# The two ends of a feed-forward's first products: token halves, order of the last transposes, and how the next product's accumulators are taken

## The chip, the cores and the metric

One core of one Trainium2 chip runs the whole program. The time is the device time of one execution in microseconds; the kernel before and the changed one compute the same function from the same inputs.

## What is computed

One layer for 512 tokens of width 1024, in float32: a mixer of four groups, a cross-attention to 256 memory rows, and a gated feed-forward of width 2816, each behind a norm and added back to x. Only the last part is touched, with the norm in front of it:

```python
def conv_glu_ffn(xn, w_up, conv_w, conv_b, w_down):
    gu = xn @ w_up                                   # 1024 -> 2 x 2816
    gate, up = jnp.split(gu, 2, axis=-1)
    gate = causal_dwconv(gate, conv_w) + conv_b      # 3 taps over the tokens
    return (jax.nn.silu(gate) * up) @ w_down         # 2816 -> 1024
...
h = conv_glu_ffn(rmsnorm(x, norm_ffn_pre[l]), ...)
x = x + rmsnorm(h, norm_ffn_post[l])
```

## The kernel before

The 512 tokens are four token tiles t of 128, the 2816 features 22 feature tiles f of 128. Every large product is done with operands split into a high and a low part (`split`, L484: a ScalarE copy that rounds to the high part, then a VectorE subtraction for the low part), three matmuls for one: high x high, high x low, low x high (`three`).

Order. Nothing in the kernel is in the order in which the code is written. Each call records an operation with an engine, a modelled cost, its dependencies and the buffers that it takes; `Plan.schedule` then lays all of them out with a greedy list scheduler, and `issue` emits them in that order. So every engine runs a fixed queue, in order, that the planner's model chose, and waits where the real times differ. The rules that matter here:

- Among the operations of an engine that are ready at the same planned time, the one with the largest `bl + boost` goes first (L275). `bl` is the longest modelled path from the operation to the end, `boost` is set by hand around pieces of code. A DMA ignores it.
- Operations stand in units (`pl.unit`). A unit starts only when the buffers that it needs can all be promised to it, and when every unit that it depends on has started (`est`, L235). PSUM has 8 banks (L40).
- A matmul into a PSUM bank depends on every earlier operation that touched that bank.

The feed-forward's norm. For each token tile t, after the cross-attention and its residual (`residual`, L1043), `norm_T` (L573) takes the squares of x on ScalarE, a power of -1/2 on GpSimd (`rr`), a scaled copy on VectorE (`xs`), eight TensorE transposes, a ScalarE copy that keeps a float32 version (`xf`), and the split into `xTh` and `xTl`. For t = 2 and 3 sums and differences of the kept tiles follow (`xf`, `Th`, `Tl`), with a boost of -60000.

First products. A feature tile is either `plain` (L1175; gate and up, 2 x 8 x 3 matmuls of 512 columns) or `seven` (L1241; a scheme of seven block products in place of eight, 7 x 12 matmuls of 256 columns, into two banks a and b, from sums of weight blocks that `blocks` forms on ScalarE and VectorE). `PLAIN` (L34) lists the plain tiles: 0, 1, 2, 6, 11, 16. Tile 0 is done by token halves: its matmuls have 256 columns, and those of the tokens of t = 0 and 1 come before those of t = 2 and 3. Tile 1 reads all four token tiles in each matmul. In a seven, S1, S3, S2 and S4 are products with sums of weight blocks, G1, G2 and U2 with plain blocks; G2 reads a bank that was first copied out (`c1`), S4 and U2 one that was copied out as `c57`. `glu` (L1164) makes the gated result `hT` from a finished tile.

Second product. Each `hT` is split into `hh` and `hl` (L1284), not before `ups[-2]`, which is what `seven(20)` returns: its product U2. The down product accumulates over the 22 feature tiles into eight banks `od[t][c]`. For f = 0 all eight stand in one unit, and its matmuls may not come before `up_`, the U2 of tile 21. The loads of x for the last residual and of the last gain wait for the same U2.

Of the kernel before, what the change touches and what calls it, by code (L numbers as in the profile page):

```python
# [30 lines left out]
NT = S // P  # L31
DFF = 2816
NF = DFF // P
PLAIN = (0, 1, 2, 6, 11, 16)  # L34
EPS = 1e-6
NEG = -1e30

# [305 lines left out]
def kernel(  # L343
# [134 lines left out]
    def tpose(o, a, idn, n=None):  # L478
        return pl.op("PE", 109.0, lambda: nc.tensor.transpose(o.ap(), a.ap(), idn.ap()), reads=[a, idn], writes=[o])  # L479
# [92 lines left out]
    @unit  # L572
    def norm_T(src, g, dst, keep=None):  # L573
        xs = [sb([P, 512], FT, "xs") for _ in range(2)]
        r = rms([src[:, h * 512:(h + 1) * 512] for h in range(2)], xs)
        for h in range(2):
            hs = slice(h * 512, (h + 1) * 512)
            stt(xs[h].all, src[:, hs], r[:, 0:1], g[:, hs], OP.mult, OP.mult)
        for h in range(2):
            p = ps([P, 4, P])  # L580
            for k in range(4):
                tpose(p[:, k, :], xs[h][:, k * P:(k + 1) * P], idn)
            if keep:
                act(keep[h], p.all, AF.Copy)
            split(*dst(h), p.all)

    def into(t):
        return lambda h: (xTh[:, t, 4 * h:4 * h + 4], xTl[:, t, 4 * h:4 * h + 4])
# [509 lines left out]
    for t in range(NT):  # L1098
# [27 lines left out]
        with pl.unit():  # L1126
            pp = []
            for c in range(2):
                p, cs = ps([P, 512]), slice(c * 512, c * 512 + 512)
                for k in range(4):  # L1130
                    wh, wl = wo[k]
                    mms(p.all, three(oh_[:, k, :], ol_[:, k, :], wh[:, 0, cs], wl[:, 0, cs]), k == 0, k == 3,
                        spare=BIG)
                pp.append(p)
            xo2 = residual(pp, g_cpost, t)
        if t < 2:
            xf.append([sb([P, 4, P], FT, "xf") for h in range(2)])
            norm_T(X[t], g_fpre, into(t), [b.all for b in xf[t]])
        else:
            with pl.unit():  # L1140
                b1, b2 = [sb([P, 4, P], FT, "xf") for h in range(2)]
                norm_T(X[t], g_fpre, into(t), [b1.all, b2.all])
                a1, a2 = xf[t - 2]
                i = t - 2
                pl.boost -= 60000.0

                tt(a1.all, b1.all, a1.all, OP.subtract)
                tt(b1.all, b2.all, b1.all, OP.subtract)
                tt(b2.all, b2.all, a1.all, OP.subtract)
                tt(a2.all, a2.all, b2.all, OP.subtract)  # L1150
                for j, v in enumerate((a1, b2, b1, a2)):
                    split(Th[j][:, i], Tl[j][:, i], v.all)
                pl.boost += 60000.0
        kept.append(store(flat(x2, t * P * D, [[D, P], [1, D]]), X[t].all, P * D * 4))


# [18 lines left out]
    def plain(f):  # L1175
        ww = [stage(wsrc(w_ffn_in, 0, KT, j * DFF + f * P, P), [P, KT, P], 8 if f < 2 else 4) for j in range(2)]
        with pl.unit():
            pp = []
            for j in range(2):
                p = ps([P, S])  # L1180
                wh, wl = ww[j]
                for hv_ in [slice(0, 2), slice(2, 4)] if f < 1 else [slice(0, 4)]:
                    for k in range(KT):
                        o = mms(p[:, hv_.start * P:hv_.stop * P],
                                three(wh[:, k, :], wl[:, k, :], xTh[:, hv_, k, :], xTl[:, hv_, k, :]),
                                k == 0, k == KT - 1)
                pp.append(p)
            glu(f, pp[0], pp[1].all)
        return o

    def raw(f):
        with pl.unit():
# [48 lines left out]
    def seven(f):  # L1241
        W = blocks(*raw(f))
        with pl.unit():
            a, b = ps([P, 2, 256]), ps([P, 2, 256])

            def prod(o, w, xs, first):
                return mms(o, [q for i in range(4) for q in three(W[w][0][i], W[w][1][i], *xs[i])], first, n=256, open_=True)
            prod(b[:, 0], "S1", tblock(0), True)
            prod(b[:, 1], "S3", tblock(2), False)
            prod(a[:, 0], "G1", xblock(0, 0), True)  # L1250
            prod(a[:, 1], "S2", tblock(1), False)
            c57 = sb([P, 2, 256], FT, "c57")
            act(c57.all, b.all, AF.Copy)
            prod(b[:, 0], "S4", xblock(1, 1), False)
            o = prod(b[:, 1], "U2", tblock(3), False)
            c1 = sb([P, 256], FT, "c1")
            act(c1.all, a[:, 0], AF.Copy)
            prod(a[:, 0], "G2", xblock(1, 0), False)
# [4 lines left out]
            tt(c57[:, 0], c57[:, 0], c57[:, 1], OP.add)  # L1263
            tt(gu[:, 768:], c1.all, c57[:, 0], OP.add)
            glu(f, gu, gu[:, S:])
        return o

    ups = [plain(f) if f in PLAIN else seven(f) for f in range(NF)]
    up_ = ups[-1]

    g_fpost = gain(norm_ffn_post, [up_])
    NL = 3
    wd, hT = [], []
    for f in range(NF):
# [6 lines left out]
            wd.append((hb.all, lb2.all))  # L1281
        with pl.unit():
            hh, hl = sb([P, S], FR, "hh", kind="hh"), sb([P, S], FR, "hl")
            act(hh.all, hP[f // 2][:, f % 2, :], AF.Copy, quota=[("hh", 4)], after=[ups[-2]])  # L1284
            tt(hl.all, hP[f // 2][:, f % 2, :], hh.all.cast(FT), OP.subtract)
            hT.append((hh, hl))

# [6 lines left out]
    od = [[ps([P, 512]) for c in range(2)] for t in range(NT)]  # L1294
    for t in range(NT):
        X[t] = sb([P, D], FT, "X2")
        load(X[t].all, flat(x2, t * P * D, [[D, P], [1, D]]), P * D * 4, after=[kept[t], up_])
    for f in range(NF - NL):
        with pl.unit():
            for t in range(NT):  # L1300
                for c in range(2):
                    down(od[t][c].all, f, t, c)
# [120 lines left out]
```

## Time and profile before

| | us |
|---|---|
| median of 3 runs (lowest to highest) | 748.5 (746.23 to 749.05) |
| the profiled execution's own time | 747.11 |
| its span, first to last instruction | 745.3 |

An execution's time is the span and what lies around it, 1.81 us here. The engines are named PE (TensorE's matmuls), PEld (its weight loads), DVE (VectorE), ACT (ScalarE), POOL (GpSimd) and SP (the queue that issues the DMAs). A matmul's recorded duration is that of a pipelined instruction; what one costs is the distance between the starts of two in a row. Line L462 is the helper `mms` for every matmul but the transposes (L479), L387 is `act`, L400 is `tt`, L412 is `stt`, L565 the power in `rms`. Tiles are told by their names: `p` is any PSUM tile, `c` is `c1` or `c57`, `su`, `sh`, `sl`, `uh` and `ul` belong to `blocks`.

### The profile page before, as it was taken

Reading aid. Unit: us, or ns where it says so; the run is one execution under the profiler, and the core shown is the slowest. Engines: PE = TensorE matmul, PEld = TensorE weight load, DVE = VectorE, ACT = ScalarE, POOL = GpSimd, SP = SyncE. Lnnn points to the kernel's source line nnn. Section 1 sums busy time; section 2 is a strip of 40 time slices with the busy share of each in tenths; the row PEclk is TensorE's granted clock in tenths of the full one; section 3 lists DMA queues with packets and bytes.
Section 4 is the critical chain, followed back from the end, with each engine's and each line's share of the span. In section 5 each row is a group of like instructions: output and inputs, shape, how many; then the busy total and the mean of one; then the engine's idle time right before and its main releaser. Section 6 shows DMA issues by size and latency. Waiting matters only on the chain.

```text
span 745.3 us, 11908 instructions
## 1 busy us (share of the span) xinstructions
PE 727.7 (98%) x4614; PEld 647.4 (87%) x4614; DVE 522.6 (70%) x1007; ACT 389.1 (52%) x790; POOL 35.5 (5%) x65
## 2 busy tenths in 40 slices
PE   7999999999999999999999999999999989999996
PEld 6898989998887988889887999999999988888885
DVE  5889956785674646676888679898979997334105
ACT  6794347546574545465666355463655565324102
POOL 3000210011000001000010000000000000000001
PEclk9999999999999999999999999999999999999999
DMA  8800320410325543333134043052234146441003
GB/s 300 299 1 1 130 93 29 173 55 28 112 116 163 163 155 103 123 113 121 51 118 166 29 142 114 29 179 77 77 126 134 34 161 235 141 150 49 0 1 113
DMA packets 25696, 82.07 MB, mean 110 GB/s; under 512 B 2980, under 2 KB 4644, under 8 KB 25640
## 3 DMA queue, kind: packets, MB, share of 16 engines
q1 hardware_dynamic: 25352, 80.72, 31.9%
q8 instruction: 36, 0.59, 0.3%
q0 software_dynamic: 288, 0.59, 0.3%
q14 instruction: 20, 0.16, 0.1%
HBM read 77.10 MB, written 4.20 MB: 109 GB/s over the span
## 4 chain that ended last, share of the span: by engine, by line
PE 85%; DVE 7%; ACT 5%; issue 2%; DMA 1%; POOL 0%; SPq 0%; DVEq 0%; POOLq 0%; ACTq 0%
PE p L462 81%; PE p L479 3%; DMA st<-in_w_in_dram 1%; PE p L474 1%; ACT wh L387 1%; DVE at L428 1%; DVE wl L400 1%; DVE Qt L400 0%; ACT e L387 0%; POOL rr L565 0%; DVE xTl L400 0%; DVE X L412 0%; DVE pg L400 0%; DVE E L400 0%; DVE sl L400 0%
## 5 line engine op out<-in xcount | busy, mean ns | idle before, releaser
L462 PE MATMUL p<-xTh,wh 128*128 128x512 f32 (+1 forms) x432 | 147.4, 341 | 2.5 <-ACT c L387 2.0
L462 PE MATMUL p<-xTl,wh 128*128 128x512 f32 (+1 forms) x432 | 145.7, 337 | 0.7 <-DVE xTl L400 0.7
L462 PE MATMUL p<-xTh,wl 128*128 128x512 f32 (+1 forms) x432 | 145.3, 336 | 0.0
L400 DVE TENSOR_TENSOR wl<-st,wh 128x1024 fp32r<-128x1024 f32 (+3 forms) x101 | 118.7, 1190 | 29.8 <-ACT wh L387 29.7
L387 ACT ACTIVATE wh<-st 128x1024 fp32r<-128x1024 f32 (+3 forms) x101 | 101.5, 1029 | 8.5 <-DMA st<-in_w_in_dram 5.8
L462 PEld LDWEIGHTS p<-xTh,wh 128*128 128x128 f32 x432 | 81.7, 189 | 10.8 <-ACT c L387 2.4
L462 PEld LDWEIGHTS p<-xTh,wl 128*128 128x128 f32 x432 | 81.7, 189 | 9.3
L462 PEld LDWEIGHTS p<-xTl,wh 128*128 128x128 f32 x432 | 81.8, 189 | 8.4 <-DVE xTl L400 1.1
L462 PE MATMUL p<-wh,xTh 128*128 128x256 f32 (+1 forms) x192 | 56.5, 294 | 0.2 <-ACT xTh L387 0.2
L462 PE MATMUL p<-wh,hh 128*128 128x512 f32 x144 | 56.7, 394 | 0.0
L462 PE MATMUL p<-wh,hl 128*128 128x512 f32 x144 | 56.7, 394 | 0.0
L462 PE MATMUL p<-wl,hh 128*128 128x512 f32 x144 | 56.7, 394 | 0.0
L462 PE MATMUL p<-wh,xTl 128*128 128x256 f32 (+1 forms) x192 | 54.0, 281 | 0.4 <-DVE xTl L400 0.4
L462 PE MATMUL p<-wl,xTh 128*128 128x256 f32 (+1 forms) x192 | 54.1, 282 | 0.0
L462 PE MATMUL p<-Th,sl 128*128 128x256 f32 x192 | 54.0, 281 | 0.0
L462 PE MATMUL p<-Th,sh 128*128 128x256 f32 x192 | 53.9, 281 | 0.0
L462 PE MATMUL p<-Tl,sh 128*128 128x256 f32 x192 | 53.9, 281 | 0.0
L400 DVE TENSOR_TENSOR hl<-hT,hh 128x512 fp32r<-128x512 f32 x22 | 15.1, 690 | 52.8 <-ACT hh L387 52.8
L387 ACT ACTIVATE hh<-hT 128x512 fp32r<-128x512 f32 x22 | 13.8, 629 | 64.2 <-PE p L462 64.2
L565 POOL TENSOR_TENSOR rr<-rv,mhalf 128x1 f32<-128x1 f32 x26 | 15.8, 608 | 568.5 <-DVE rv L407 565.0
L462 PEld LDWEIGHTS p<-wh,xTh 128*128 128x128 f32 x192 | 36.2, 189 | 1.0 <-ACT xTh L387 0.5
L400 DVE TENSOR_TENSOR pg<-p,gain 128x512 f32<-128x512 f32 x24 | 16.4, 685 | 29.1 <-ACT sq L387 29.1
(281 smaller groups left out, 1760.9 us busy)
## 6 DMA issues: line engine op xcount, KB each, us to landing
st<-in_w_ffn_in_dram SPq DMA_DIRECT2D x44, 512.0 KB, 4.5
st<-in_w_in_dram SPq DMA_DIRECT2D x24, 512.0 KB, 4.3
st<-in_w_ffn_out_dram SPq DMA_DIRECT2D x22, 512.0 KB, 3.7
st<-in_w_mix_out_dram SPq DMA_DIRECT2D x8, 512.0 KB, 4.6
st<-in_w_ck_dram SPq DMA_DIRECT2D x4, 512.0 KB, 9.1
st<-in_w_cv_dram SPq DMA_DIRECT2D x4, 512.0 KB, 3.9
X<-in_x_dram SPq DMA_DIRECT2D x4, 512.0 KB, 3.9
st<-in_w_cq_dram SPq DMA_DIRECT2D x4, 512.0 KB, 3.9
```

The source lines that it names most:

```text
L387: return nc.scalar.activation(o.ap(), i.ap(), func, **kw)
L400: return pl.op(eng, c, lambda: e.tensor_tensor(o.ap(), a.ap(), b.ap(), op=op), reads=[a, b], writes=[o], fifo=fifo, boost=boost)
L428: return pl.op("DVE", dcost(n, True), lambda: nc.vector.copy_predicated(o.ap(), m.ap(), a.ap()), reads=[m, a, o], writes=[o])
L462: i = nc.tensor.matmul(o.ap(), l.ap(), r.ap(), start=first and j == 0, stop=last and j == len(terms) - 1, skip_group_check=open_)
L474: i = nc.tensor.matmul(o[hh * 64:hh * 64 + 64].ap(), l.ap(), r.ap(), start=j == 0, stop=j == len(terms) - 1)
L479: return pl.op("PE", 109.0, lambda: nc.tensor.transpose(o.ap(), a.ap(), idn.ap()), reads=[a, idn], writes=[o])
L565: pl.op("Pool", 470.0, lambda: nc.gpsimd.tensor_tensor(r.all.ap(), v.all.ap(), mhalf[:, :1].ap(), op=OP.pow), reads=[v.all, mhalf.all], wr ...
```

## The change

- `PLAIN` is 0, 1, 2, 6, 11, 17: tile 17 is plain and tile 16 a seven.
- Tile 1 is also done by token halves.
- In `norm_T` the split comes ahead of the kept copy. (Only the feed-forward's norm keeps one.)
- The feed-forward's `norm_T` of every token tile is recorded with a boost of +5000, where it had -5000 t.
- `seven` and `plain` return two products; of a seven, S1 and U2. `hh` waits for the S1 of tile 21 (was: the U2 of tile 20), and the down product's first matmuls for the S1 of tile 21 (was: its U2). The loads still wait for its U2.
- The down product's f = 0 has a unit for each of the eight accumulators, where it had one for all.

```diff
-PLAIN = (0, 1, 2, 6, 11, 16)
+PLAIN = (0, 1, 2, 6, 11, 17)
...
+            split(*dst(h), p.all)
             if keep:
                 act(keep[h], p.all, AF.Copy)
-            split(*dst(h), p.all)
...
             xo2 = residual(pp, g_cpost, t)
+        pl.boost = 5000.0
         if t < 2:
             xf.append([sb([P, 4, P], FT, "xf") for h in range(2)])
             norm_T(X[t], g_fpre, into(t), [b.all for b in xf[t]])
...
-                pl.boost -= 60000.0
+                pl.boost = -60000.0
...
-                pl.boost += 60000.0
...
-                for hv_ in [slice(0, 2), slice(2, 4)] if f < 1 else [slice(0, 4)]:
+                for hv_ in [slice(0, 2), slice(2, 4)] if f < 2 else [slice(0, 4)]:
...
-            prod(b[:, 0], "S1", tblock(0), True)
+            o = prod(b[:, 0], "S1", tblock(0), True)
...
-            o = prod(b[:, 1], "U2", tblock(3), False)
+            e = prod(b[:, 1], "U2", tblock(3), False)
...
-        return o
+        return o, e
...
-    up_ = ups[-1]
-
-    g_fpost = gain(norm_ffn_post, [up_])
+    up_, upe = ups[-1]
+
+    g_fpost = gain(norm_ffn_post, [upe])
...
-            act(hh.all, hP[f // 2][:, f % 2, :], AF.Copy, quota=[("hh", 4)], after=[ups[-2]])
+            act(hh.all, hP[f // 2][:, f % 2, :], AF.Copy, quota=[("hh", 4)], after=[up_])
...
-        load(X[t].all, flat(x2, t * P * D, [[D, P], [1, D]]), P * D * 4, after=[kept[t], up_])
-    for f in range(NF - NL):
+        load(X[t].all, flat(x2, t * P * D, [[D, P], [1, D]]), P * D * 4, after=[kept[t], upe])
+    for t in range(NT):
+        for c in range(2):
+            down(od[t][c].all, 0, t, c)
+    for f in range(1, NF - NL):
```

## Rows read from the trace of the kernel before

**Rows 1.** The page's first part: busy time of each engine in us, its share of the span, and instructions.

```profile
PE 727.7 (98%) x4614; PEld 647.4 (87%) x4614; DVE 522.6 (70%) x1007; ACT 389.1 (52%) x790; POOL 35.5 (5%) x65
```

**Rows 2.** The chain that ended last, in order of time, from 374 to 400 us and from 585 us to the end: start, length, what. The order of the rows is that of time.

```profile
381.31 0.70 ACT sq L387 x2
...
386.80 1.54 POOL rr L565
...
391.62 0.70 DVE xTl L400
...
614.46 0.39 ACT c L387
...
614.90 119.97 PE p L462 x522
```

**Rows 3.** Busy time by windows of 10 us: the window, its length, then busy us (and instructions) of PE, PEld, DVE, ACT and POOL, the granted clock of TensorE, the DMA engines' share and GB/s.

```profile
370.00:380.00 10.00, 10.00 (x61) 8.52 (x60) 8.30 (x16) 6.96 (x20) 1.28 (x3) 1.00 0.13 54
380.00:390.00 10.00, 9.17 (x70) 8.38 (x69) 8.22 (x15) 5.27 (x15) 2.08 (x2) 1.00 0.38 119
390.00:400.00 10.00, 8.69 (x40) 6.97 (x41) 9.61 (x16) 6.96 (x12) 0.00 (x0) 0.83 0.90 354
600.00:610.00 10.00, 8.51 (x71) 8.25 (x70) 9.76 (x14) 8.83 (x16) 0.00 (x0) 1.00 0.29 80
```

**Rows 4.** PE in order of time, end of the first halves of tile 0, transposes of t = 3, first matmuls of tile 1 (512 columns), second halves of tile 0 from 395.63 on: start, recorded length, line, operation, out<-in, in brackets the idle time before it and what ended it.

```profile
387.70 0.28 PE L462 MATMUL p<-xTl,wh 128*128 128x256 f32 x1
...
388.18 0.28 PE L462 MATMUL p<-xTh,wl 128*128 128x256 f32 x1
389.26 1.29 PE L479 MATMUL p<-ident,xs 128*128 128x128 f32 x8 [0.79 <-DVE xs L412]
391.12 0.50 PE L462 MATMUL p<-xTh,wh 128*128 128x512 f32 x1 [0.57 <-ACT xTh L387]
392.36 0.79 PE L462 MATMUL p<-xTl,wh 128*128 128x512 f32 x1 [0.74 <-DVE xTl L400]
392.95 0.63 PE L462 MATMUL p<-xTh,wl 128*128 128x512 f32 x1
393.38 0.63 PE L462 MATMUL p<-xTh,wh 128*128 128x512 f32 x1
...
395.63 0.28 PE L462 MATMUL p<-xTh,wh 128*128 128x256 f32 x1
```

**Rows 5.** PE in order of time at the other end: last matmuls of the product before it, then G2 of tile 20 (604.04), S1 of tile 21 (605.58); G2 of tile 21 (614.90) and the first matmul of the down product (616.43).

```profile
602.27 0.28 PE L462 MATMUL p<-Th,sl 128*128 128x256 f32 x1
604.04 0.39 PE L462 MATMUL p<-xTh,wh 128*128 128x256 f32 x1 [1.49 <-ACT c L387]
...
605.58 0.28 PE L462 MATMUL p<-Th,sh 128*128 128x256 f32 x1
...
614.14 0.28 PE L462 MATMUL p<-Th,sl 128*128 128x256 f32 x1
614.90 0.39 PE L462 MATMUL p<-xTh,wh 128*128 128x256 f32 x1 [0.47 <-ACT c L387]
...
616.43 0.40 PE L462 MATMUL p<-wh,hh 128*128 128x512 f32 x1
616.66 0.39 PE L462 MATMUL p<-wl,hh 128*128 128x512 f32 x1
```

**Rows 6.** PE in order of time: the transposes of t = 2 and, behind them, the first matmul of tile 0.

```profile
381.74 1.04 PE L479 MATMUL p<-ident,xs 128*128 128x128 f32 x8
382.53 0.36 PE L462 MATMUL p<-xTh,wh 128*128 128x256 f32 x1
```

**Rows 7.** DVE in order of time from 386.6 us: sums and splits of the kept tiles (`xf`, `Tl`), and the low parts of t = 3 (`xTl`).

```profile
386.63 0.69 DVE L400 TENSOR_TENSOR xf<-xf,xf 128x512 f32<-128x512 f32 x1
387.23 0.69 DVE L400 TENSOR_TENSOR Tl<-xf,Th 128x512 fp32r<-128x512 f32 x1
...
391.62 1.28 DVE L400 TENSOR_TENSOR xTl<-p,xTh 128x512 fp32r<-128x512 f32 x2
```

**Rows 8.** ACT in order of time, from 381 us: the copies of t = 3 out of PSUM.

```profile
389.98 0.60 ACT L387 ACTIVATE xf<-p 128x512 f32<-128x512 f32 x1 [3.67 <-PE p L479]
390.48 0.59 ACT L387 ACTIVATE xTh<-p 128x512 fp32r<-128x512 f32 x1
```

**Rows 9.** All instructions that read or write `rr` between 300 and 400 us, by line: durations in ns, smallest, median and largest, then first and last start.

```profile
L565 POOL TENSOR_TENSOR rr<-rv,mhalf x12: 548/548/1527, 304.4 to 386.8; 128x1 f32<-128x1 f32 x12
```

**Rows 10.** Waits of PE between 330 and 383 us: engine, line, what it waited for: us in total, times, longest.

```profile
PE p L462 <- DVE ol L400: 1.2, 1, 1.2
```

**Rows 11.** ACT in order of time from 600 us.

```profile
601.55 0.62 ACT L387 ACTIVATE hh<-hT 128x512 fp32r<-128x512 f32 x1
...
603.11 0.61 ACT L387 ACTIVATE hh<-hT 128x512 fp32r<-128x512 f32 x1
```

**Rows 12.** DVE in order of time from 600 us.

```profile
602.75 0.68 DVE L400 TENSOR_TENSOR hl<-hT,hh 128x512 fp32r<-128x512 f32 x1
...
605.09 0.68 DVE L400 TENSOR_TENSOR sl<-su,sh 128x512 fp32r<-128x512 f32 x1
```

**Rows 13.** Busy time by windows, columns as in Rows 3.

```profile
400.00:600.00 200.00, 200.00 (x1482) 190.24 (x1481) 172.51 (x274) 107.56 (x181) 0.00 (x0) 1.00 0.27 90
588.00:614.00 26.00, 24.51 (x198) 23.86 (x197) 25.07 (x40) 15.93 (x27) 0.00 (x0) 1.00 0.38 122
```

More of the change, by code (lines that the diff above doesn't have):

```diff
@@ L1188, in plain @@
             glu(f, pp[0], pp[1].all)
-        return o
+        return o, o
     def raw(f):
@@ L1265, in seven @@
             glu(f, gu, gu[:, S:])
-        return o
+        return o, e
     ups = [plain(f) if f in PLAIN else seven(f) for f in range(NF)]
-    up_ = ups[-1]
-    g_fpost = gain(norm_ffn_post, [up_])
+    up_, upe = ups[-1]
+    g_fpost = gain(norm_ffn_post, [upe])
     NL = 3
```

## The prediction

> **What bounds the kernel now.** First the page's busy times: PE is busy for 727.7 of the span's 745.3 us, no other engine for more than 70% [rows 1]. So time can be gained only where PE waits or runs slowly, and the page's average doesn't say where. Second the chain of waits in order of time: from 392 us on it is PE's own matmuls but for a piece around 600 us and the last residual, and its longest piece, 119.97 us, runs without a break through the whole down product [rows 2]. That says that between 392 and 735 us only matmul work counts, save at two places. Third the windows: PE is full in 370 to 380, short of work in 380 to 400 and in 600 to 610, and 390 to 400 is the one early window with a granted clock under 1, 0.83 [rows 3]. Fourth PE in order of time at these two places, which gives their price.
>
> First end. Tile 0's first halves end at 388.18 + 0.12 = 388.30 (0.12 us is the distance of 256-column matmuls, four of them from 387.70 to 388.18) and the second halves begin at 395.63 [rows 4]. These 7.33 us hold eight transposes (0.79 for eight, from 381.74 to 382.53 [rows 6]) and nine 512-column matmuls at 0.23 (616.43 to 616.66 [rows 5]), 2.07. Lost: 7.33 - 0.79 - 2.07 = 4.47 us. Three waits make most of it: for `xs`, for `xTh`, for `xTl` [rows 4]. The rest is clock: from 392.95 to 393.38 one such matmul takes 0.43, against 0.23 above, the lower of the two levels, 1.2 GHz [rows 4, 5].
>
> Second end. G2 of tile 20 starts at 604.04 and could at 602.39; from there to S1 of tile 21 it takes 1.54, not 12 x 0.12 = 1.44. G2 of tile 21 starts at 614.90 and could at 614.26; to the down product it takes 1.53 [rows 5]. Lost: 1.65 + 0.10 + 0.64 + 0.09 = 2.48 us, both times for the copy `c1` on ACT [rows 2, 5].
>
> Both together are 6.95 us, 0.9% of the time; no part of this change can reach more by its own account. A kernel that is within 0.5% (3.7 us) can't be told from no change here.
>
> **The change part by part.**
>
> **Token halves for tile 1.** Removed: 48 matmuls of 512 columns; added: 96 of 256. Cost: 48 x (2 x 0.12 - 0.23) = 0.48 us, all of it on PE, so on the path. Moved: 48 of them, 48 x 0.12 = 5.76 us, need only t = 0 and 1, and can run in the hole of 4.47 us. Do they have their weights? Tile 1's first matmul runs at 391.12, ahead of tile 0's second halves, and it waited for `xTh` alone [rows 4]; so yes. PE then has 5.76 + 5.76 + 0.79 = 12.3 us of work behind 382.53, to 394.8; the last low part of t = 3 is written at 391.62 + 1.28 = 392.9 [rows 7]. Cover: 1.9 us. It also ends what made the clock fall: PE no longer stands still three times within four microseconds, and the 1.65 us at 602.39 show that one such stop left the clock at 1.00 [rows 3, 5].
>
> **Transposes ahead, split ahead of the kept copy.** With a boost of +5000 in place of -15000, the transposes of t = 3 go ahead of the rest of the first halves as soon as the planner holds them for ready. That is the part that can give back: PE works its queue in order, so if `xs` is later than planned, the halves behind the transposes wait too. How late? The chain from the last cross-attention matmul (about 381.75) to the first transpose took 7.5 us [rows 4, 6]; adding up the kernel's own planned costs of the same steps gives about 6.0, and this only fixes the place in the queue. One step is visibly the culprit: the power on GpSimd took 1.53 us at 386.80, where the median of the twelve around it is 0.55 [rows 2, 9]. Bounds of the stall that stays: 0 if that step takes 0.55 and the rest is as planned, 1.5 if all is as in this trace. I take 1.0, near the one excess of 0.98 that a row shows. The split ahead of the kept copy moves `xTh` forward by one ACT copy, 390.48 - 389.98 = 0.5 us [rows 8]; with the cover above it is worth nothing by itself, and 0.5 if the cover fails. The kept copies come later by the same; they feed only the sums for the sevens. No DMA is issued by any of this, and on SP only the store of x behind the residual moves with its data.
>
> The 1.53 us may be a collision. At that time DVE ran two subtractions with both inputs in SBUF, at 386.63 and 387.23, while the power was due; they end at 387.92, and the power at 388.33 [rows 2, 7]. The Trainium skill, page "SBUF — State Buffer", section "SBUF: two separate sides", says that GpSimd and a VectorE instruction with two SBUF inputs take a shared port pair as an exclusive lock, the other blocking for the whole instruction; the trace agrees, with 1.53 us for 0.55. By that rule the change leaves the collision in place, since the same low-priority subtractions still fill DVE's pause there, and the stall stays at about 1.0; without it the sum would be 1.0 better.
>
> **Boost for all token tiles.** The norm of t = 1 and 2 now goes ahead of the cross-attention of later tiles on ACT, DVE and PE. Nothing in this trace shows that order. PE waited there for one operand only, 1.2 us [rows 10], and was full in 370 to 380 [rows 3]. Bounds: a gain of 0.5 (the transposes of t = 2 and their copies are out of the way of t = 3) and a loss of 2 (some four ACT or DVE steps of 0.5 fall on the path of t = 3). I take 0, as PE is full.
>
> **Tile 17 plain for 16, hh after S1 of 21.** No matmul more or less: six plain and sixteen seven, as before. The wait at 604.04 ended with a `c1` copy that stood behind two `hh` copies of 0.6 on ACT, and DVE had an `hl` of 0.68 in the same stretch [rows 11, 12]; `hh` now waits for S1 of tile 21, so these leave the place. That gives 1.0. The rest of the 1.65 is DVE: the first low part that S1 of tile 21 needs starts at 605.09 and ends at 605.77 [rows 12], and DVE is busy for 25.07 of the 26 us from 588 to 614 [rows 13]. Taking the two `hh` away alone would move the wait from G2 to S1. Here tile 17 matters: the plain tile's matmuls are what the planner puts where a seven's weights are late, and one tile later they reach tiles 20 and 21. Of 1.75 (wait and slower matmuls) I take 1.3, bounds 0.6 (the `hl` alone) and 1.75.
>
> **Accumulators one by one.** G2 of tile 21 waits for its own product's copy, 0.64 us with nothing else to run, since all eight accumulators had to be free together. Six banks are free at that time, so f = 0 matmuls of six accumulators (18 x 0.23 = 4.1 us) can run there. Of 0.73 I take 0.6. It isn't free: what ran ahead can't cover the release of banks a and b after the last product, which in this trace passed unseen, as 616.43 follows without a wait [rows 5]. Bounds: +0.73, and -1.0.
>
> Sum: 4.47 - 1.0 - 0.48 + 0 + 1.3 + 0.6 = 4.9 us gained. From the profiled execution's 747.11 that is 742.2. The four executions known (746.23, 747.11, 748.5, 749.05) have their middle at 747.8, 0.7 above the profiled one, and the median shown is another 0.7 higher; I put the forecast at 747.8 - 4.9 = 742.9.
>
> **Rivals.**
>
> 1. *The first end stays where it is: PE queues behind the early transposes.* For it: the 1.53 us above, and 7.5 us of chain where 6.0 were planned. If the whole 1.5 stays as a stall, another wait like that for `xTh` (0.57) follows, and 0.48 is paid, the first end gives 1.9 and the whole 3.1 at half of the other: 747.8 - 2.9 = 744.9. Against it: 1.9 us of cover behind the transposes. Chance 0.22.
> 2. *VectorE becomes the bound.* PE, 3 us ahead from 395 on, asks for weights of the sevens earlier; DVE is busy for 172.51 of the 200 us from 400 to 600 [rows 13]. If it can't follow, the gain of the first end is paid back as waits for `sl`: only the second end and what little fits remain, 747.8 - 2 = 745.8. Against it: DVE has 27 us of pauses there, and PE none. Chance 0.12.
> 3. *Slower: the boost delays the cross-attention of t = 3.* The last low part `xTl` hangs on it, and PE has no work to put in its place before 381.7, since tile 0's halves are queued behind. Each norm put ahead has six ACT steps of about 0.6 [rows 8], 3.6 us. If two of them fall on that path, 7 us are added before the first halves, and the most that the rest can give is 6.5: 747.8 + 0.5 to 751. It decides from 4.9 us of delay on. Against it: ACT and DVE have 3 and 1.7 us of pauses in 370 to 380 [rows 3]. Chance 0.08.
> 4. *All of it comes back.* The power takes 0.55, the plain matmuls fill the second end: 4.47 - 0.48 + 2.48 = 6.5, 741.3. Chance 0.13.
>
> The forecast has 0.45.
>
> **How the numbers follow.** The range leaves out no more than 2 in 10: from the full recovery on the fastest execution (746.23 - 6.5 = 739.7) to rivals 1 and 2 on the slow executions (745.8 + 1.4, and the lower part of rival 3): 739.7 to 748.4. Faster by over 0.5% means below 744.8: most of the forecast (0.42), rival 4 (0.13) and a part of rival 1 (0.06): 0.61. Slower by over 0.5% means above 752.2: the far part of rival 3, 0.04. Within: 0.35.
>
> **What would show it.** Right: 96 matmuls of 256 columns on PE behind the transposes of t = 2, no idle time over 0.3 us between the transposes of t = 3 and the second halves, a granted clock of 1.00 in all windows from 380 to 400, no `hh` ahead of the last `c1` copies, and down matmuls between the products of tile 21. Wrong: an idle piece of PE over 1.5 us in front of the transposes of t = 3 (rival 1), idle pieces between 400 and 600 us that end with `sl` (rival 2), or a last cross-attention matmul later than 384 us (rival 3).

## The result and the profile after

The changed kernel takes 743.25 us (median of 4 runs, 743.12 to 744.28), the kernel before 748.54 in the same job (4 runs, 746.23 to 749.05): a ratio of 0.9943, 95% interval [0.9922, 0.9964]. So it is faster, by 0.57% in the middle and by 0.36% at the interval's near end. The forecast was 742.9, range 739.7 to 748.4. The profiled execution of the changed kernel took 743.27 us with a span of 741.5, 3.8 below the profiled one of before (747.11 and 745.3). Left out of every number below is one execution of down_low that took 1442.68 us, where its five others took 742.18 to 742.79.

The page's first part (columns as in [rows 1]): PE has 48 more matmuls and is busy for 726.1 us.

```profile
PE 726.1 (98%) x4662; PEld 648.2 (87%) x4662; DVE 523.9 (71%) x1007; ACT 390.5 (53%) x790; POOL 35.0 (5%) x65
```

Windows of the changed kernel (columns as in [rows 3]).

```profile
380.00:390.00 10.00, 10.00 (x76) 9.34 (x75) 9.22 (x18) 6.97 (x16) 0.55 (x1) 1.00 0.13 46
390.00:400.00 10.00, 10.00 (x87) 10.00 (x86) 8.42 (x14) 5.40 (x9) 0.99 (x1) 1.00 0.99 378
600.00:610.00 10.00, 9.42 (x65) 8.57 (x64) 10.00 (x16) 5.82 (x10) 0.00 (x0) 1.00 0.57 160
610.00:620.00 10.00, 9.49 (x58) 8.09 (x57) 8.23 (x12) 4.66 (x7) 0.00 (x0) 1.00 0.96 346
```

The first end is full, 10.00 of 10 us in both windows, where [rows 3] had 9.17 and 8.69, and its clock stays at 1.00, where it fell to 0.83. The second end is not: 9.42 and 9.49. DVE is busy for all of 600 to 610.

PE in order of time at the first end of the changed kernel, to be held against [rows 4, 6]: the transposes of t = 2 inside the last cross-attention products, the first of the first halves, the transposes of t = 3, the halves behind them.

```profile
380.42 0.61 PE L479 MATMUL p<-ident,xs 128*128 128x128 f32 x4
...
381.56 0.60 PE L479 MATMUL p<-ident,xs 128*128 128x128 f32 x4
...
383.38 0.28 PE L462 MATMUL p<-xTh,wh 128*128 128x256 f32 x1
...
391.94 0.60 PE L479 MATMUL p<-ident,xs 128*128 128x128 f32 x4
...
392.73 0.60 PE L479 MATMUL p<-ident,xs 128*128 128x128 f32 x4
393.09 0.36 PE L462 MATMUL p<-xTh,wh 128*128 128x256 f32 x1
```

No row has a wait in brackets. Between 383.38 and 391.94 stand 72 of the 96 first halves (8.56 / 72 = 0.119 us each). The transposes are in the queue behind three quarters of the halves, and `xs` is ready just in time, as the rows of DVE show; the rows of POOL have the power before it. (Both: start, length, in brackets the idle time before.)

```profile
389.94 0.69 DVE L400 TENSOR_TENSOR Tl<-xf,Th 128x512 fp32r<-128x512 f32 x1
391.07 1.41 DVE L412 SCALAR_TENSOR_TENSOR xs<-X,rr,gain 128x512 f32<-128x512 f32 x2 [0.45 <-POOL rr L565]
```

```profile
385.59 0.55 POOL L565 TENSOR_TENSOR rr<-rv,mhalf 128x1 f32<-128x1 f32 x1 [6.12 <-DVE rv L407]
390.04 0.99 POOL L565 TENSOR_TENSOR rr<-rv,mhalf 128x1 f32<-128x1 f32 x1 [3.90 <-DVE rv L407]
```

The first `xs` ends near 391.07 + 0.74 = 391.8, some 0.1 us before its transposes start. The power is still long, 0.99, with a subtraction of two SBUF tiles beside it, but now nobody waits for it.

In exchange there is a small wait in the cross-attention (PE in order of time).

```profile
375.95 1.16 PE L462 MATMUL p<-cpt,cv 128*128 128x128 f32 x8 [0.24 <-ACT cpt L387]
```

The second end, PE in order of time, to be held against [rows 5]: the last three matmuls of plain tile 17, S1 of tile 21, the down product's first matmuls, S4 (`xTh,sh`) of tile 21, and the last two accumulators of f = 0.

```profile
599.92 0.39 PE L462 MATMUL p<-xTh,wh 128*128 128x512 f32 x1
...
600.61 0.28 PE L462 MATMUL p<-Th,sh 128*128 128x256 f32 x1
...
601.59 0.39 PE L462 MATMUL p<-Th,sl 128*128 128x256 f32 x1 [0.58 <-DVE sl L400]
...
607.13 0.39 PE L462 MATMUL p<-wh,hh 128*128 128x512 f32 x1
...
611.29 0.28 PE L462 MATMUL p<-xTh,sh 128*128 128x256 f32 x1
...
615.88 0.50 PE L462 MATMUL p<-wh,hh 128*128 128x512 f32 x1 [0.19 <-DVE c L400]
...
617.18 0.47 PE L462 MATMUL p<-wh,hh 128*128 128x512 f32 x1 [0.32 <-DVE gu L400]
```

The waits for `c1` are gone; 18 down matmuls run from 607.13 to 611.29 between the products of tile 21, as foretold. In their place come a wait for `sl` and two holes at the last two accumulators.

**Where the time went.** One sum serves all kernels below. Take each matmul's distance from the start of the one before, less what it is in an unbroken row (0.119 us for 256 columns, 0.233 for 512, 0.11 for 128), and add up what is over 15 ns; waits, the slow start behind them and a low clock all count. Starts up to 335 us differ by up to 2.1 us between executions of the same instructions, so spans are taken from PE's wait for `ol` ([rows 10]; it ends at 334.79 before, 334.84 after).

| us lost by PE | cross-attention | first end | second end | span from 335 |
|---|---|---|---|---|
| before | 1.28 | 4.44 | 2.61 | 410.55 |
| changed | 2.01 | 0.33 | 1.87 | 406.62 |

First end +4.1, cross-attention -0.7, second end +0.7, and the halves themselves 48 x (2 x 0.119 - 0.233), about -0.25: 3.9, and the spans differ by 3.93.

The medians differ by more, 5.3, and what is over goes with TensorE's clock. Of the 70 executions of the kernel before that were timed beside the experiments, the 15 with the highest mean granted clock, 0.999, took 744.91 to 746.57 us (median 745.8); the 32 with 0.995 or less took 747.41 to 749.80. Three of the changed kernel's four executions have 0.998 and took 743.12 to 743.27. With the clock kept on both sides the change is thus worth about 2.6 us, an estimate from these medians of different jobs.

### The profile page after: what moved, and what is told of

Same layout as the page of the kernel before. It is cut to its first block, busy times and chain, and to the rows that moved or that the text cites. A ratio compares the mean times of both kernels' runs of the same rounds, so it can differ in the third digit from the quotient of the medians.

```text
span 741.5 us, 12007 instructions
## 1 busy us (share of the span) xinstructions
PE 726.1 (98%) x4662; PEld 648.2 (87%) x4662; DVE 523.9 (71%) x1007; ACT 390.5 (53%) x790; POOL 35.0 (5%) x65
## 4 chain that ended last, share of the span: by engine, by line
PE 86%; DVE 7%; ACT 4%; issue 1%; DMA 1%; SPq 0%; POOL 0%; DVEq 0%; POOLq 0%; ACTq 0%
PE p L462 82%; PE p L479 3%; DMA st<-in_w_in_dram 1%; DVE wl L400 1%; PE p L474 1%; ACT wh L387 1%; DVE at L428 1%; DVE Qt L400 0%; ACT e L387 0%; SPq L371 0%; DVE E L400 0%; DVE hl L400 0%; ACT hqb L387 0%; DVE lo L400 0%; DVE X L412 0%
## 5 line engine op out<-in xcount | busy, mean ns | idle before, releaser
L462 PE MATMUL p<-xTh,wh 128*128 128x256 f32 (+1 forms) x448 | 149.3, 333 | 0.0
L462 PE MATMUL p<-xTl,wh 128*128 128x256 f32 (+1 forms) x448 | 147.6, 330 | 0.0
L462 PE MATMUL p<-xTh,wl 128*128 128x256 f32 (+1 forms) x448 | 147.5, 329 | 0.0
L462 PEld LDWEIGHTS p<-xTh,wl 128*128 128x128 f32 x448 | 84.4, 188 | 8.4
L462 PEld LDWEIGHTS p<-xTh,wh 128*128 128x128 f32 x448 | 84.4, 188 | 6.8 <-issue 0.2
L462 PEld LDWEIGHTS p<-xTl,wh 128*128 128x128 f32 x448 | 84.4, 188 | 6.6
L462 PEld LDWEIGHTS p<-Th,sl 128*128 128x128 f32 x192 | 36.2, 189 | 0.8 <-DVE sl L400 0.8
```

The source lines that it names most:

```text
L462: i = nc.tensor.matmul(o.ap(), l.ap(), r.ap(), start=first and j == 0, stop=last and j == len(terms) - 1, skip_group_check=open_)
```

## Experiments

Theory A: each part acts at its own place, as the two traces show it, and the places add up. Theory B is a rival of its own in each expectation. Each kernel was timed in 5 rounds beside the kernel before, whose medians in the three jobs were 747.22, 747.68 and 748.06. Columns as above.

| kernel | us | ratio to before | cross-att. | first end | second end | span from 335 |
|---|---|---|---|---|---|---|
| undo_ahead | 745.9 | 0.999 [0.9979, 1.0002] | 1.27 | 4.19 | 1.88 | 409.82 |
| undo_halves | 754.67 | 1.0101 [1.0083, 1.0119] | 2.00 | 6.85 | 5.68 | 417.16 |
| undo_tile17 | 746.2 | 0.9987 [0.9975, 0.9999] | 2.01 | 0.33 | 3.73 | 408.51 |
| undo_down | 743.43 | 0.9956 [0.9939, 0.9972] | 2.01 | 0.33 | 1.59 | 406.41 |
| boost_t3 | 746.67 | 0.9986 [0.9973, 0.9999] | 1.27 | 0.55 | 5.69 | 409.59 |
| plain18 | 750.07 | 1.0036 [1.0024, 1.0048] | 2.00 | 0.33 | 7.71 | 413.35 |
| down_low | 742.64 | 0.9934 [0.9915, 0.9954] | 2.01 | 0.33 | 0.85 | 405.29 |
| no_clash | 747.06 | 0.9993 [0.9979, 1.0008] | 1.27 | 2.36 | 2.57 | 408.54 |
| first_only | 747.18 | 0.9991 [0.9982, 1.0] | 2.00 | 0.33 | 5.91 | 410.54 |
| second_only | 749.84 | 1.0027 [1.0016, 1.0039] | 1.27 | 3.14 | 5.70 | 412.44 |
| best_t23 | 742.05 | 0.9919 [0.9905, 0.9932] | 1.35 | 0.31 | 0.83 | 404.85 |
| best_t23_p18 | 742.11 | 0.992 [0.9906, 0.9933] | 1.35 | 0.33 | 0.70 | 404.89 |

**undo_ahead.** The changed kernel with the old order of the norm.

```diff
-            split(*dst(h), p.all)
             if keep:
                 act(keep[h], p.all, AF.Copy)
+            split(*dst(h), p.all)
...
-        pl.boost = 5000.0
...
-                pl.boost = -60000.0
+                pl.boost -= 60000.0
...
+                pl.boost += 60000.0
```

> The changed kernel without its transposes ahead: boost of the feed-forward's norm back to -5000 t, kept copy ahead of the split; halves of tile 1, tile 17 and the down part stay. In PE's queue the transposes of t = 3 then stand behind all 96 matmuls of 256 columns, and the cross-attention is in the order of the kernel before. Theory A (both parts are needed): the transposes start near 382.5 + 96 x 0.119 = 394.0; in the kernel before the second matmul that needs the low part came 3.1 us behind their start, 0.8 of it the transposes themselves, so PE stands still for 2.3 us; the last cross-attention matmul is 0.85 us earlier than in the changed kernel. Net 1.5 us slower than the changed kernel, span 743.0. Rival B (the halves alone close the hole, the boost only costs): no such wait, span 740.6, 0.9 faster than the changed kernel.

PE in order of time around the transposes of t = 3 in this kernel, then one of its windows.

```profile
394.99 1.04 PE L479 MATMUL p<-ident,xs 128*128 128x128 f32 x8
397.31 0.38 PE L462 MATMUL p<-xTh,wh 128*128 128x256 f32 x1 [1.29 <-ACT xTh L387]
398.46 0.39 PE L462 MATMUL p<-xTl,wh 128*128 128x256 f32 x1 [0.77 <-DVE xTl L400]
```

```profile
400.00:410.00 10.00, 10.00 (x60) 9.33 (x59) 7.97 (x12) 6.98 (x9) 0.00 (x0) 0.85 0.01 5
```

The transposes come behind all 96 halves, so the copies behind them find nothing to hide them: 2.06 us of waits, and a window at a clock of 0.85. The first end loses 4.19, nearly the 4.44 of before, though tile 1 is in halves. A is right on the place and too small in size, since it counted the waits and not the clock. This profiled execution is the slowest of its twelve (747.50 at a mean clock of 0.995; median 745.9, fastest 745.14 at 0.999), so not every one pays that clock. The run takes back the boost and the place of the split together: of the 1.29 before `xTh`, about 0.5 is the kept copy [rows 8]. The cross-attention is back at 1.27: the boost made the 0.73 there.

**undo_halves.** The changed kernel with tile 1 in one piece.

```diff
-                for hv_ in [slice(0, 2), slice(2, 4)] if f < 2 else [slice(0, 4)]:
+                for hv_ in [slice(0, 2), slice(2, 4)] if f < 1 else [slice(0, 4)]:
```

> The changed kernel with tile 1 in matmuls of 512 columns again; all else stays. Theory A (the halves of tile 1 are what fills the hole): PE runs out of work 48 x 0.119 = 5.7 us behind the first half, near 389.1, and the transposes of t = 3 have their data only near 391.9: idle 2.8 us, then another 2 us for the low parts, and a granted clock under 1 again; 0.3 us of matmul overhead comes back. 4 to 6 us slower than the changed kernel, span 745.5 to 747.5. Rival B (the earlier transposes closed the hole): at most 1 us slower.

PE in front of the transposes of t = 3, then the window.

```profile
392.88 1.84 PE L479 MATMUL p<-ident,xs 128*128 128x128 f32 x8 [2.64 <-DVE xs L412]
```

```profile
390.00:400.00 10.00, 7.17 (x24) 5.07 (x23) 8.69 (x16) 5.55 (x12) 0.99 (x1) 0.68 1.00 378
```

This is rival 1 of the prediction: PE stands in front of the early transposes, 2.64 us, and the clock falls to 0.68 in the window. The boost without the halves costs 2.4 us more at this end than both together undone, and the halves without the boost give next to nothing: each needs the other. The second end is worse too, 5.68, which A didn't expect; in all the kernel is 10.5 us slower than the changed one by the trace, where A said 4 to 6.

**undo_tile17.**

```diff
-PLAIN = (0, 1, 2, 6, 11, 17)
+PLAIN = (0, 1, 2, 6, 11, 16)
```

> The changed kernel with tile 16 plain instead of 17; all else stays. Theory A (VectorE sets the start of S1 of tile 21, and the plain tile's left-over matmuls only fill in front of it): no matmul of the plain tile is left there, so the wait for the low part sl, 0.85 us in the changed kernel, grows by the three 512-column matmuls that stood in front of it, 0.7 us: span 742.2. Rival B (the two hh copies out of the way were all of it): no difference over 0.3 us.

PE in order of time, S1 of the last two tiles (both 256 columns).

```profile
592.16 0.39 PE L462 MATMUL p<-Th,sl 128*128 128x256 f32 x1 [0.36 <-DVE sl L400]
...
603.90 0.39 PE L462 MATMUL p<-Th,sl 128*128 128x256 f32 x1 [1.56 <-DVE sl L400]
```

The wait is for `sl`, the sums' low parts, as A has it, but the loss is 1.9 us, not 0.7: more than one tile waits.

**undo_down.** f = 0 in one unit again, behind U2 of tile 21.

```diff
-            after=[up_] if f == 0 else [])
+            after=[upe] if f == 0 else [])
...
-    for t in range(NT):
-        for c in range(2):
-            down(od[t][c].all, 0, t, c)
-    for f in range(1, NF - NL):
+    for f in range(NF - NL):
```

> The changed kernel with f = 0 of the down product again as one unit of eight accumulators behind U2 of tile 21; hh still waits for S1 of tile 21. Theory A (running ahead only moves the hole): G2 of tile 21 waits for its copy again, 0.7 us, and the two waits at the start of the last accumulators, 0.45 and 0.48 us in the changed kernel, go: 0.2 us faster than the changed kernel, span 741.3. Rival B (as predicted, the accumulators one by one give 0.6 us): 0.6 us slower, span 742.1.

All waits of PE from 599 to 620, in order of time.

```profile
602.69 0.39 PE L462 MATMUL p<-Th,sl 128*128 128x256 f32 x1 [0.58 <-DVE sl L400]
611.72 0.39 PE L462 MATMUL p<-xTh,wh 128*128 128x256 f32 x1 [0.47 <-ACT c L387]
```

The wait for `c1` is back (as [rows 5] had it at 614.90), and both holes at the last two accumulators are gone. Net 0.2 us by the trace in favour of the old way; the times of the two can't be told apart. Taking the accumulators one by one, as the change does it, gains nothing.

**down_low.** The changed kernel, with the early matmuls of f = 0 last in line among what is ready.

```diff
+    pl.boost = -8000.0
     for t in range(NT):
...
+    pl.boost = 0.0
```

> The changed kernel with a boost of -8000 for the f = 0 matmuls of the down product, so that they stand behind the products of tile 21 instead of between them; each accumulator still has its own unit. Theory A (running ahead used up the cover for the release of the last two banks): the waits of 0.45 and 0.48 us at the start of the last two accumulators go, and nothing comes in their place, since S2 covers the copy in front of S4 and S4 the one in front of G2: 0.9 us faster than the changed kernel. Rival B (the down matmuls between were needed to cover these copies): waits of 0.5 to 1.5 us inside tile 21, no gain.

All waits of PE from 412 to 640 us: engine, line, what it waited for, us in total, times, longest.

```profile
PE p L462 <- DVE sl L400: 0.6, 1, 0.6
```

Only the wait for `sl` is left, and 1.0 us is gained on the changed kernel at the second end, 1.3 by the spans (A: 0.9). So the idea of the edit was right; what spoiled it is that six accumulators were filled at 607, while products of tile 21 were ready, and nothing was left to fill the end.

**no_clash.** The kernel before, with the sums of the kept tiles behind the last `xs`, so that no DVE subtraction of two SBUF tiles runs beside the power.

```diff
-                norm_T(X[t], g_fpre, into(t), [b1.all, b2.all])
-                a1, a2 = xf[t - 2]
...
+                seen = norm_T(X[t], g_fpre, into(t), [b1.all, b2.all])
+            xf.append((b1, b2))
...
+            pl.boost = -60000.0
+            tt(a1.all, b1.all, a1.all, OP.subtract, after=[seen])
+            tt(b1.all, b2.all, b1.all, OP.subtract, after=[seen])
```

> The kernel before with one thing else: the sums of the kept tiles (xf, Th, Tl of t = 2) wait for the last xs of t = 3, so that VectorE runs no subtraction with two SBUF inputs while the power on GpSimd is due. Theory A (that is what made the power take 1.53 us in place of 0.55): it takes 0.55, the transposes come about 1.0 us earlier, and the kernel is 1.0 us faster than the one before, if the sums, now later, aren't missed by the first seven. Rival B (the power is slow there for another reason): 1.0 to 1.5 us as before, no gain.

The instructions that touch `rr` from 375 to 400 us (as [rows 9]), then PE in order of time, then the window.

```profile
L565 POOL TENSOR_TENSOR rr<-rv,mhalf x3: 550/551/551, 378.1 to 386.5; 128x1 f32<-128x1 f32 x3
```

```profile
388.46 1.03 PE L479 MATMUL p<-ident,xs 128*128 128x128 f32 x8
390.78 0.49 PE L462 MATMUL p<-xTh,wh 128*128 128x512 f32 x1 [1.29 <-ACT xTh L387]
391.74 0.50 PE L462 MATMUL p<-xTl,wh 128*128 128x512 f32 x1 [0.46 <-DVE xTl L400]
```

```profile
390.00:400.00 10.00, 8.76 (x47) 7.38 (x48) 9.65 (x17) 6.63 (x12) 0.00 (x0) 1.00 0.84 339
```

The power takes 0.55 where it took 1.53, the wait for `xs` is gone, the clock stays at 1.00, and the first end loses 2.36 for 4.44. So the long power was a collision. It is not worth the whole 2.1: second_only (further down) has the first end of the kernel before, with the same three stops (0.80, 0.57, 0.74), and there the clock stayed at 1.00 too.

```profile
392.61 0.50 PE L462 MATMUL p<-xTl,wh 128*128 128x512 f32 x1 [0.74 <-DVE xTl L400]
```

```profile
390.00:400.00 10.00, 8.65 (x48) 7.02 (x47) 9.60 (x17) 7.00 (x12) 0.00 (x0) 1.00 0.90 360
```

It loses 3.14 at the first end. So the collision costs 3.14 - 2.36 = 0.8 us, and the other 1.3 of the kernel before is a fall of the clock that the same stops don't bring in every execution. The times (0.9993, its interval over 1) don't separate no_clash from the kernel before.

**boost_t3.** The changed kernel, with the boost for t = 3 alone.

```diff
-        pl.boost = 5000.0
+        pl.boost = 5000.0 if t == 3 else -5000.0 * t
```

> The changed kernel with the boost of +5000 for the norm of t = 3 alone; t = 0 to 2 keep -5000 t. All else stays. Theory A (the boost of t = 1 and 2 put their norms into the path of the last cross-attention): the three small waits of PE near 371 and 377 us, 0.73 us together beyond the kernel before, go; the transposes of t = 3 stand behind 54 matmuls in place of 72 and wait for at most 0.5 us. PE's queue at the other end is another one too, with no matmul of the plain tile left in front of S1 of tile 21, so the wait for sl there grows, by up to the 1.9 us of the run with tile 16 plain. From the cross-attention to the start of the sevens 0.3 to 0.7 us gained; in all between 0.7 faster and 1.5 slower than the changed kernel. Rival B (the boost isn't what delays the cross-attention): first matmul of tile 0 as late as in the changed kernel, 48.5 us behind the wait near 335.

PE's waits at its second end, in order of time.

```profile
592.17 0.38 PE L462 MATMUL p<-Th,sl 128*128 128x256 f32 x1 [0.68 <-DVE sl L400]
...
604.29 0.39 PE L462 MATMUL p<-Th,sl 128*128 128x256 f32 x1 [1.95 <-DVE sl L400]
...
621.44 0.48 PE L462 MATMUL p<-wh,hh 128*128 128x512 f32 x1 [0.78 <-DVE gu L400]
```

The cross-attention's 0.73 is back and the first end stays at 0.55, as A says. Yet the kernel is 3.0 us slower than the changed one by the trace: the second end, 200 us later, loses 5.69 for 1.87. What differs there is where the matmuls of plain tile 17 stand. Groups of PE's instructions by form, one of the three alike groups of 512 columns: the changed kernel from 585 to 605 us, then boost_t3 from 555 to 585.

```profile
L462 PE MATMUL p<-xTh,wh 128*128 128x512 f32 x4 | 1.6, 394 | 0.0
```

```profile
L462 PE MATMUL p<-xTh,wh 128*128 128x512 f32 x17 | 6.7, 393 | 0.0
```

A plain tile has 48 of them, so three of the 51 in boost_t3 are left from tile 11. From 585 to 605 boost_t3 has no such matmul at all. The changed kernel keeps 3 x 4 = 12 for the last two tiles, nine in front of tile 20 and three in front of tile 21. The scheduler lays out the whole program anew, so a boost at 375 us has used up the filling by 585.

**plain18.** Tile 18 plain in place of 17.

```diff
-PLAIN = (0, 1, 2, 6, 11, 17)
+PLAIN = (0, 1, 2, 6, 11, 18)
```

> The changed kernel with tile 18 plain instead of 17. Theory A (VectorE is the bound in the last sevens, and what counts is how many matmuls of the plain tile are left to stand in front of S1 of tile 21: 18 instead of 3, 4.2 us for 0.7): the wait for sl there, 0.85 us, goes, nothing else changes: 0.8 us faster than the changed kernel. Rival B (six sevens in a row before the plain tile, 12 to 17, bring the same wait there): 0 to 1 us slower.

PE's waits from 600 us, in order of time.

```profile
601.69 0.39 PE L462 MATMUL p<-Th,sh 128*128 128x256 f32 x1 [0.72 <-ACT sh L387]
...
605.76 0.58 PE L462 MATMUL p<-Th,sl 128*128 128x256 f32 x1 [3.56 <-DVE sl L400]
```

B is right, and by more than it said: 6.7 us slower than the changed kernel by the trace (0.85 of it is a wait for `sl` at 560 us, outside the columns). Both waits stand in S1 of tile 21, with 18 matmuls of the plain tile right in front of it, so A's count of these matmuls does not decide the wait. A later plain tile isn't better by itself.

**first_only and second_only.** The changed kernel with the second end of before (the diff, and f = 0 in one unit as in undo_down); the kernel before with the second end of the change (its edits of `PLAIN`, `hh`, `up_` and f = 0, no others).

```diff
-PLAIN = (0, 1, 2, 6, 11, 17)
+PLAIN = (0, 1, 2, 6, 11, 16)
...
-    up_, upe = ups[-1]
+    up_, upe = ups[-1][1], ups[-1][1]
...
-            act(hh.all, hP[f // 2][:, f % 2, :], AF.Copy, quota=[("hh", 4)], after=[up_])
+            act(hh.all, hP[f // 2][:, f % 2, :], AF.Copy, quota=[("hh", 4)], after=[ups[-2][1]])
```

> The kernel before with the first end of the change alone: token halves for tile 1, split ahead of the kept copy, boost of +5000. Tile 16 plain, hh behind U2 of tile 20 and the eight accumulators in one unit as before. Theory A (the ends are independent): 4.1 us of holes go, 0.3 of matmul overhead and 0.7 in the cross-attention come, the second end keeps its 2.6 us: 3.1 us faster than the kernel before. Rival B (PE, 4 us ahead, meets VectorE in the last sevens, and the gain comes back there as waits for sl, as in the run with tile 16 plain, with the hh copies on top): second end 4.5 to 6 us, in all 1 us faster to 1 us slower than the kernel before.

> The kernel before with the second end of the change alone: tile 17 plain for 16, hh behind S1 of tile 21, accumulators one by one. Tile 1 in 512 columns, boost and order of the norm as before. Theory A (independent): second end 1.9 us in place of 2.6, the first end as before: 0.7 us faster than the kernel before. Rival B (which plain matmuls are left for the end depends on the first end too: in the run without the halves none was left in front of S1 of tile 21, and the second end lost 5.7 us): 3 us slower.

The longest wait of PE at the second end: first_only, then second_only.

```profile
603.37 0.39 PE L462 MATMUL p<-xTh,wh 128*128 128x256 f32 x1 [2.43 <-ACT c L387]
```

```profile
606.19 0.39 PE L462 MATMUL p<-Th,sl 128*128 128x256 f32 x1 [1.92 <-DVE sl L400]
```

B in both by size; but in first_only the longest wait is for `c1`, not for `sl`, as B had it, and second_only is 1.9 us slower than before, not 3, since its first end kept the clock (3.14). The first end's gain is whole in first_only (0.33 left of 4.44) and is paid back at the second (5.91 for 2.61). The second end's edits without the first make the kernel 0.27% slower. Theory A, that the places add up, falls here: alone they give -0.0 and +1.9 us of span from 335, together -3.9.

**best_t23, best_t23_p18.** The changed kernel with down_low's edit and the boost for t = 2 and 3 alone; then the plain tiles 0, 1, 2, 6, 13, 18 too.

```diff
-        pl.boost = 5000.0
+        pl.boost = 5000.0 if t > 1 else -5000.0 * t
```

> The changed kernel with two things else: boost of +5000 for the norm of t = 2 and 3 alone (t = 0 and 1 keep -5000 t), and a boost of -8000 for the f = 0 matmuls of the down product. Theory A (the boost of t = 1 is what delays the last cross-attention, that of t = 3 or 2 is what the halves need, and the queue at the second end stays that of the changed kernel with 3 matmuls in front of S1 of tile 21): cross-attention 0.7 us shorter, second end 0.9 us as in the run with low down matmuls: 1.7 us faster than the changed kernel, 0.7 faster than that run. Rival B (any other boost shifts the queue, as the boost for t = 3 alone did): second end 3 us or more, slower than the changed kernel.

> As the run before it, with the plain tiles 0, 1, 2, 6, 13, 18 for 0, 1, 2, 6, 11, 17: six sevens in a row between 6 and 13, four between 13 and 18, three behind 18. Theory A (what made tile 18 slow was six sevens just in front of the last plain tile, not the tile's place): waits for sl of at most 1 us in all, 2.0 us faster than the changed kernel. Rival B (a plain tile later than 17 leaves VectorE behind whatever stands before it): waits of 3 us or more, as with tile 18 and 11.

All waits of PE in best_t23 from 334 us to the end (columns as above).

```profile
PE p L462 <- DVE ol L400: 1.2, 1, 1.2
PE p L462 <- DVE sl L400: 0.6, 1, 0.6
```

A is right for both: the 0.7 of the cross-attention and the 1.0 of the holes are gained. At 0.9919 [0.9905, 0.9932] of the kernel before this is the lowest ratio found, though the interval of down_low overlaps it; the other plain tiles change nothing more.

## Why the prediction was right, step by step

The time and the direction were right; the sum of 4.9 was 3.9 by the traces, and the terms under it were off on both sides of the sum. The forecast came nearer (743.25 for 742.9) by luck: the prediction raised its base by 0.7 over the profiled execution, 747.11, for the spread of the kernel before. The changed kernel's executions lie close together, its median at its profiled 743.27, so the raise had no counterpart and hid 0.7 of the 1.0 by which the sum was too large. Rival 1's price has a slip, 3.1 gained but 2.9 taken off; it changes nothing here.

- **First end, 4.47 lost, 1.0 to stay.** The price was right (4.44 by the sum over all matmuls). The term mis-sized is the stall in front of the transposes: 1.0 was taken, nothing came. The power did stay long, 0.99, so the step on the cause held. The Trainium skill, page "SBUF — State Buffer", section "SBUF: two separate sides", has GpSimd and a VectorE instruction with two SBUF inputs take a shared port pair as an exclusive lock. The traces agree with it in both directions: 0.99 beside a subtraction with two SBUF inputs, 0.55 in no_clash without one. What failed is the step from a late power to a stall of PE. The transposes were put behind 72 halves, 8.56 us of work, and those cover it. The prediction had the halves as cover behind the transposes and none before them. The margin is 0.1 us: undo_halves shows what the same boost costs without the halves.
- **Halves, 0.48.** Measured about 0.25. The prediction took 0.12 and 0.23 from starts printed to 0.01 us; over 72 halves it is 0.119, and since 0.24 and 0.23 are nearly equal, that rounding is half of their difference.
- **Clock.** Right for the changed kernel: 1.00 from 380 to 400. Of the 4.1 us it is about 1.3 (4.44 before, 3.14 in second_only with the same stops and the clock at 1.00). The prediction took the fall for a consequence of the three stops; second_only shows that they don't always bring it.
- **Boost for all token tiles, 0.** It cost 0.73, within the bounds (+0.5 to -2): first waits of PE for ACT in 370 to 377. Rival 3 happened in this size, not in the 7 us that it needed: the first FFN matmul comes 0.85 us later (383.38 for 382.53). undo_ahead and boost_t3, without it, lose 1.27 there, best_t23, with t = 2 still boosted, 1.35: so the boost of t = 0 and 1 makes nearly all of it.
- **Split ahead of the kept copy.** Counted at nothing with the cover; not tried by itself.
- **hh and tile 17, 1.3.** The wait for `c1` at tile 20 is gone, as foretold, and moved to S1 of tile 21, 0.58 for `sl`, as was feared there. One sign named for it did not come: two `hh` copies, at 602.45 and 602.97, still stand ahead of the `c1` of tile 21 at 607.34, but nothing waits for that copy. By the trace 1.65 + 0.10 became the 0.85 us that down_low still has: 0.9, in the bounds of 0.6 to 1.75. That tile 17 matters is shown by undo_tile17 (1.9 us).
- **Accumulators one by one, 0.6.** This term failed: 0.73 of wait went, and the two holes at the last two accumulators (0.45 and 0.48 with the slow matmul behind) came, the event that the bound of -1.0 named. undo_down puts it at -0.2. With a low priority (down_low) it gives the foretold gain.
- **Rival 2, VectorE becomes the bound.** Not between 400 and 600, where no wait of PE is listed; but at 600 to 610 DVE is busy for 10.00 of 10, and PE's wait for `sl`, 0.58, lies there. In the experiments the longest waits for `sl`, 1.56 to 3.56 us, lie between 603 and 612, in S1 of tile 21; shorter ones, to 0.72, come a tile earlier, and plain18 has one at 560. The rival had the right engine, mostly at the wrong place.

The prediction missed what the experiments showed most clearly: it treated the two ends as separate terms of a sum. Both edits move the whole plan, and the second end's loss ran from 0.70 to 7.71 us over the twelve kernels tried, where the prediction had reckoned with the 2.48 of the kernel before.

What stays open is the rule by which the second end comes out well. In undo_ahead, undo_down, down_low and best_t23, as in the changed kernel, matmuls of tile 17 are left for the last two tiles, and the loss is under 2; in boost_t3, second_only and undo_halves none are, and it is 5.7. But plain18 has 18 right in front of tile 21 and loses 7.71, and best_t23_p18 has none so late and loses 0.70. So the place of the plain matmuls goes with it and doesn't decide it alone; it can't be told from these runs what in DVE's order does.

## What to carry to other kernels

Where a planner lays out all queues, an edit at one place has its price at every place where the plan is tight: look at all of PE's waits after it, not at the edited stretch, and judge an edit in the company of the others, not by itself. Work that needs only early operands (token halves) pays when it stands in front of the late instruction in the queue; an order that moves the late instruction forward without such work makes a stall of it. Filling a later hole with early work needs a low priority, or the filling is used up before the hole.

## What the runs showed of the hardware

- A power of 128 x 1 on GpSimd took 1.53 us beside two DVE subtractions of 128 x 512 with both inputs in SBUF, 0.99 us beside one, and 0.55 alone (before, changed, no_clash). Both times it ended 0.40 us behind the last such subtraction (388.33 for 387.92, 391.03 for 390.63), as if it started when that was over. Beside a DVE product of a PSUM and an SBUF tile (changed kernel, 385.43 to 386.11; the power at 385.59) it took 0.55. So small an instruction can thus delay a chain by 1 us.
- The clock didn't follow the stops alone. Stops of 0.79, 0.57 and 0.74 us [rows 4] were followed by matmuls at the lower level, 1.2 GHz, and a window at 0.83; stops of 0.80, 0.57 and 0.74 us in second_only, in the same instructions, left it at 1.00. 1.29 and 0.77 us in undo_ahead were followed by a window at 0.85; 1.29 and 0.46 us in no_clash left it at 1.00, as did 1.49 at the second end of before and 1.56 in undo_tile17. All six longer stops between 380 and 620 us went with a fall: 1.92 (second_only), 1.94 (undo_halves), 1.95 (boost_t3) and 2.43 us (first_only) with a window at 0.83 or 0.84, 2.64 us (undo_halves) with 0.68 and 3.56 us (plain18) with 0.66.
- The clock's share of a loss is large: in boost_t3 the three waits are 0.68 + 1.95 + 0.78 = 3.41 us, and the loss is 5.69; the other 2.3 us are slow matmuls behind them. About 1.7 of that is the clock, an estimate from the window 600 to 610 (10 us at 0.83).
